# A hybrid encoder step on one core: the forget gate's running sums issued beside the first gate projection's blocks, and dense turns at 0.941 a step

## The chip, the cores and the metric

The kernel runs on one core of a Trainium2 chip. The metric is the device time of one execution in microseconds (us), lower is better. Before the change three runs took 1885.36, 1890.35 and 1894.71 us; the median is 1890.35 us.

The engines of the core appear under the names that the profile gives them: PE (matrix multiply, with PEld for its weight loads), DVE (vector), ACT (activation), POOL (the fourth compute engine) and SP, which here only starts DMAs. Each engine works off its own list of instructions in order; what one needs from another it waits for.

## The reference, cut to what matters

One layer of an encoder over 1024 prompt rows and 8 x 16 rows of running streams with 1024 cached rows each. All heads read one normalised input `u` through one combined projection:

```python
proj = jnp.einsum('bnd,de->bne', u, p['w_in'])
sq, sk, sv, fq, fk, fv, fg, z, xbc, dt = split_last(proj, IN_SIZES)
logf = jax.nn.log_sigmoid((fg + p['fox_b_f']).astype(jnp.float32))
# stick-breaking attention on sq, sk, sv
# forgetting attention ("FoX") on fq, fk, fv:
fcum = jnp.cumsum(logf, axis=1)                                     # prompt
fcum = jnp.cumsum(jnp.concatenate([past['fox_logf'], logf], axis=1), axis=1)   # streams
s = s + (fq_cum[..., :, None] - fk_cum[..., None, :])               # added to the scores before the softmax
# state-space mixer ("SSD") on z, xbc, dt; its output is gated:
ssd_o = rmsnorm(y * jax.nn.silu(z), p['ssd_norm_g'])
mix = jnp.concatenate([sb_o, fox_o, ssd_o], axis=-1)
out = jnp.einsum('bne,ed->bnd', mix, p['w_out'])
```

A cross-attention into 256 memory rows, a SwiGLU feed-forward and a last norm follow. The new keys, values, log gates and states are returned too. What the change touches is the running sum `fcum` of the log forget gates, and the time at which it is computed beside the projection of `z`.

## The kernel before, in words

A projection in this kernel is made of fp32 numbers split in a high and a low part; one product is three matmuls (`mm3`, L328, L329, L330). A block of weights is loaded by SP (L317) into a ring of four buffers `wr`, cast to its high part `wh` by ACT (L292), and its low part `wl` is subtracted by POOL in pieces of 256 columns (`pool_tt`, L132). L329 is the matmul of the three that reads `wl` in the projections whose weights are the moving operand.

Up to about 95 us of the span the kernel projects the memory rows and normalises the input; the first projections follow. From about 125 us to about 700 us runs the mixed stage, in which this change lies. It is written as generators that yield after a piece of work, a *turn*:

- `pipeline` (L629, called at L1297) makes one *step* for each unit of attention, 112 steps in all: 56 of stick-breaking attention, then 56 of FoX attention. A prompt unit of stick-breaking makes scores in pieces of up to 512 columns (PE L560, L561, and L563 for the mask), two sigmoids of each (ACT L519, L520), a running product over the whole row (DVE scan L522) and a product of the two (POOL L132, pieces of 256 columns, named `ws<-ws`). One step later the row is transposed (PE L578) and multiplied with the values (L593). A decode unit, for the running streams, loads cached keys (SP L882, into the same ring `wr`), transposes them (L888), multiplies (L873, L901, L902), and later transposes its weights (L924) and multiplies with the cached values (L933, L956).
- `fill_s` makes the *dense* turns: projections of FoX's queries and keys (12 turns; their matmuls have 384 columns), of its values and the forget gate (FV, 9 turns, 260 columns), the running sums (`fox_sums`, 4 turns), then what the list `ORD` names: `z0`, the first half of the gate z with dt (9 turns, 264 columns), `dt` (1), the xbc projection (24), and `z1` (9). That is 68 turns.
- At every step, `RATE[0]` is added to a counter and one dense turn is issued for each whole number in it (1.0 before). When the dense turns are used up, the SSD mixer's turns follow at `RATE[1]` = 1.1 a step.

The order in which the code issues instructions isn't yet the order on the engines: a scheduler sorts them for each engine by priority and by a model of when they could start. A step that is issued elsewhere can so move its instructions on all five engines.

`fox_sums` starts when FV has written the log gates' inputs `lf`. DVE and ACT compute the log of the gate (L400 to L413, L658), SP stores it (L660, L661) and loads the cached gates (L665), POOL makes three masks of ones and zeros in a buffer `sg` (L667 to L674), PE sums along the rows with them (L682, L683), transposes the sums (L690), sums over the chunks of the cache (L705 to L707) and spreads the result (L725). The sums go to memory (L692, L716, L718) and are read by the first FoX head and by the `z1` entry of `fill_s`, much later. PE's results lie in `psd`, a pool of two buffers, which FV's, z0's and xbc's blocks use too. `pad_cols` loads and transposes three old rows of the convolution's input (L782, L785); the first xbc turn reads them.

## Time and profile before

| | before |
|---|---|
| median of three runs | 1890.35 us |
| the profiled execution | 1894.55 us |
| its span | 1892.8 us |
| mean granted PE clock | 0.988 |
| PE busy | 97% of the span |
| DVE, ACT, POOL busy | 47%, 42%, 33% |
| DMA queues' share of 16 engines | 49.6% |

The profile is of one execution. Times in the timeline are counted from the span's start. A timeline row gives the start, the duration, the engine, the line, the operation with its tiles (out<-in), its shape and a count of equal instructions run together; in brackets stand the idle time ahead of it and what ended it. A table by windows gives for each stretch its width, the busy time and count of instructions of PE, PEld, DVE, ACT and POOL, then the granted PE clock (1.00 is full), the busy share of the DMA engines and GB/s. A fp32 matmul that isn't of the split kind is counted twice by the profile and once in the lists of the order below.

### The profile page before, as it was taken

The page shows a single profiled execution, that of the slowest core. Times are in us where ns is not written, and L with a number is a line of the kernel's source. Part 1 is how long each engine was busy: PE and PEld are TensorE (multiplying, and loading weights), DVE is VectorE, ACT ScalarE, POOL GpSimd, SP SyncE. Part 2 cuts the span into 40 slices and gives each one's busy share as a digit, 9 for nine tenths or more (in the row PEclk, how much of TensorE's full clock was granted, in tenths as well). Part 3 has the DMA queues.
Part 4 walks back from the last instruction along what each step waited for, and adds up shares of the span by engine and source line. Part 5 has one row for each costly group of instructions (what it writes and reads, how often), then busy time and mean ns, then how long its engine had stood idle before and what let it go on. Part 6 is the DMA issues. An engine that isn't in the chain of part 4 may idle for free.

```text
span 1892.8 us, 32368 instructions
## 1 busy us (share of the span) xinstructions
PE 1837.7 (97%) x12136; PEld 1638.6 (87%) x12136; DVE 886.4 (47%) x1798; ACT 802.1 (42%) x1719; POOL 617.9 (33%) x921
## 2 busy tenths in 40 slices
PE   7999999999999989999999989999999999999998
PEld 5899778888967767899988889999999999888886
DVE  3412323475656863444444586333333333455554
ACT  6522544545455862344332374333333333344443
POOL 7622425445115673111112107444444542000000
PEclk9999999999989999999999999999999999999999
DMA  9465654437587883245576124233322223657572
GB/s 338 145 189 149 206 142 133 147 109 207 179 249 228 282 290 102 108 134 173 173 271 219 56 81 112 75 87 79 76 71 70 70 70 105 207 187 243 174 243 89
DMA packets 291068, 296.64 MB, mean 157 GB/s; under 512 B 80092, under 2 KB 242884, under 8 KB 290912
## 3 DMA queue, kind: packets, MB, share of 16 engines
q1 hardware_dynamic: 290912, 294.57, 49.6%
q8 instruction: 96, 1.57, 0.3%
q14 instruction: 60, 0.49, 0.1%
HBM read 225.12 MB, written 69.91 MB: 156 GB/s over the span
## 4 chain that ended last, share of the span: by engine, by line
PE 83%; DMA 5%; DVE 4%; POOL 3%; ACT 3%; issue 2%; SPq 0%; DVEq 0%; POOLq 0%; ACTq 0%
PE psd L1868 11%; PE psd L328 10%; PE psd L329 10%; PE psd L330 10%; PE pst L1868 8%; PE pss L1868 4%; PE pss L328 3%; PE pss L330 3%; PE pss L329 3%; PE pso L1868 2%; POOL wl L132 2%; PE pst L328 1%; PE pst L329 1%; PE pst L330 1%; PE pso L593 1%
## 5 line engine op out<-in xcount | busy, mean ns | idle before, releaser
L132 POOL TENSOR_TENSOR wl<-wr,wh 128x256 fp32r<-128x256 f32 (+2 forms) x184 | 142.1, 805 | 233.0 <-ACT wh L292 232.8
L328 PE MATMUL psd<-act,wh 128*128 128x384 f32 x528 | 182.3, 345 | 0.0
L330 PE MATMUL psd<-act,wl 128*128 128x384 f32 x528 | 181.1, 343 | 0.6 <-POOL wl L132 0.6
L329 PE MATMUL psd<-act,wh 128*128 128x384 f32 x528 | 181.7, 344 | 0.0
L1868 PE MATMUL pst<-bT,tr 128*128 128x256 f32 (+1 forms) x1068 | 155.0, 293 | 0.0
L1868 PEld LDWEIGHTS pst<-bT,tr 128*128 128x128 f32 x1068 | 144.9, 188 | 0.1
L330 PE MATMUL psd<-wh,act 128*128 128x512 f32 (+3 forms) x424 | 136.9, 324 | 0.0
L329 PE MATMUL psd<-wl,act 128*128 128x256 f32 (+3 forms) x414 | 134.2, 325 | 2.7 <-POOL wl L132 2.7
L328 PE MATMUL psd<-wh,act 128*128 128x256 f32 (+3 forms) x414 | 133.3, 326 | 1.4 <-DMA act<-osc 1.0
L1868 PE MATMUL psd<-bT,tr 128*128 128x320 f32 (+1 forms) x912 | 132.8, 295 | 0.7 <-POOL tr L132 0.7
L1868 PEld LDWEIGHTS psd<-bT,tr 128*128 128x128 f32 x912 | 124.7, 188 | 1.0 <-POOL tr L132 0.9
L132 POOL TENSOR_TENSOR tr<-u,tr 128x256 fp32r<-128x256 f32 x110 | 82.6, 779 | 101.7 <-ACT tr L1704 83.8
L253 POOL TENSOR_SCALAR sm<-sm 128x1 f32<-128x1 f32 (+2 forms) x27 | 9.1, 338 | 297.3 <-ACT y L1970 207.8
L1843 DVE TENSOR_TENSOR tr<-tr,pst 128x256 f32<-128x256 f32 (+1 forms) x86 | 38.6, 449 | 139.9 <-ACT tr L1840 106.6
L330 PEld LDWEIGHTS psd<-act,wl 128*128 128x128 f32 x528 | 99.2, 188 | 3.2 <-issue 1.9
L132 POOL TENSOR_TENSOR ws<-ws 128x256 f32<-128x256 f32 (+2 forms) x100 | 69.3, 721 | 98.1 <-DVE ws L522 83.9
L328 PEld LDWEIGHTS psd<-act,wh 128*128 128x128 f32 x528 | 99.4, 188 | 2.2 <-issue 1.8
L329 PEld LDWEIGHTS psd<-act,wh 128*128 128x128 f32 x528 | 99.3, 188 | 1.9 <-issue 1.5
L132 POOL TENSOR_TENSOR tr<-raw,tr 128x256 fp32r<-128x256 f32 x94 | 69.2, 765 | 83.9 <-ACT tr L1704 75.7
L1704 ACT CAST tr<-tr 128x384 fp32r<-128x384 f32 (+1 forms) x70 | 37.6, 538 | 123.0 <-DMA tr<-hidsc 117.3
L329 PEld LDWEIGHTS psd<-wl,act 128*128 128x128 f32 x414 | 79.2, 191 | 10.9 <-POOL wl L132 4.0
L292 ACT CAST wh<-wr 128x512 fp32r<-128x512 f32 (+2 forms) x90 | 52.5, 622 | 81.7 <-PE psd L330 32.0
(643 smaller groups left out, 4730.5 us busy)
## 6 DMA issues: line engine op xcount, KB each, us to landing
u<-w_down SPq DMA_DIRECT2D x40, 512.0 KB
raw<-w_down SPq DMA_DIRECT2D x26, 512.0 KB
st<-qksc SPq DMA_DIRECT2D x48, 256.0 KB
wr<-w_in SPq DMA_DIRECT2D x44, 256.0 KB
tr<-hidsc SPq DMA_DIRECT2D x57, 192.0 KB
hidsc<-tr SPq DMA_DIRECT2D x34, 288.0 KB
qksc<-sg SPq DMA_DIRECT2D x48, 192.0 KB
wr<-cache_sb_k SPq DMA_DIRECT2D x32, 256.0 KB
```

Of the source, the lines that this page charges most:

```text
L132: POOL.tensor_tensor(out=out[:, a0:a1], in0=in0[:, a0:a1], in1=in1[:, a0:a1], op=op)
L253: POOL.tensor_scalar(v, ss, inv, EPS, ALU.mult, ALU.add)
L292: ACT.copy(hi, raw)
L328: PE.matmul(out, ah, bh, start=start, stop=False)
L329: PE.matmul(out, ah, bl, start=False, stop=False)
L330: PE.matmul(out, al, bh, start=False, stop=stop)
L593: return PE.matmul(po[r:r + 64, q_], vt[:, 2 * (k0 + i) + j, :], pfs[i][:, sl], start=start and k0 == 0 and (j == 0 or qp > 0), stop=k0 + ...
L1704: ACT.copy(hi, src)
L1843: DVE.tensor_tensor(out=at(out, g), in0=at(x, g), in1=ps[g][:, :GW[g]], op=op)
L1868: PE.matmul(dst[g][:, :GW[g]], x[:, ka], y[:, k, :], start=start and k == 0 and m == 0, stop=stop and k == 3 and m == 2, skip_group_check= ...
```

## The change

The dense rate goes from 1.0 to 0.941 turns a step. The running sums are no longer four turns of their own between FV and z0. They become a generator `sums`, and `beside` issues one of its turns behind each of the first four turns of z0. What is left of it (nothing, since z0 has nine turns) and `pad_cols` are issued ahead of the first xbc turn. There are now 64 dense turns, 4 fewer, and 64/68 = 0.941, so that the last of them falls on about the step it fell on before.

```diff
-RATE = (1.0, 1.1, 60)
+RATE = (0.941, 1.1, 60)
...
         yield from proj_v(1, C_FV, p_v[1], s_v[1], extra=4)
-        yield from fox_sums()
-        pad_cols()
+        sums = fox_sums()
+
+        def beside(gen):
+            for _ in gen:
+                next(sums, None)
+                yield
         for o in ORD:
...
             if o[0] == "z":
-                yield from z_proj(int(o[1]))
+                yield from beside(z_proj(int(o[1])))
             elif o == "dt":
                 dt_softplus()
                 yield
             else:
+                drain(sums)
+                pad_cols()
                 yield from xbc_proj(*o)
```

No instruction is added or taken away. The lists of the engines differ between about 150 us and 450 us of the span of before, a little between about 577 us and 705 us, and hardly anywhere else.

The first place is PE's list where FV begins. Rows read: line, operation, tiles out<-in, shape, and a count. `psd<-act,..` of 384 columns are the last turns of the projections ahead of FV, `psd<-wh,act` and `psd<-wl,act` of 260 columns are FV; `pst<-ident,ws` and `pso<-` belong to a decode unit, `pss<-` are scores. Before:

```order
L471 MATMUL pst<-ident,pt 128x128
L924 MATMUL pst<-ident,ws 128x128 x8
L471 MATMUL pst<-ident,pt 128x128 x2
L560 MATMUL pss<-st 128x128
L561 MATMUL pss<-st 128x128
L563 MATMUL pss<-mask_sb,identr 128x128
L560 MATMUL pss<-st 128x256
L561 MATMUL pss<-st 128x256
L563 MATMUL pss<-mask_sb,identr 128x128
L328 MATMUL psd<-wh,act 128x260
L924 MATMUL pst<-ident,ws 128x128
```

And with the change, from the last 384-column matmul on (the eight L924 stand 28 rows further up, and 24 matmuls of 384 columns and the ninth L924 between):

```order
L330 MATMUL psd<-act,wl 128x384
L560 MATMUL pss<-st 128x128
L561 MATMUL pss<-st 128x128
L563 MATMUL pss<-mask_sb,identr 128x128
L560 MATMUL pss<-st 128x256
L561 MATMUL pss<-st 128x256
L563 MATMUL pss<-mask_sb,identr 128x128
L933 MATMUL pso<-pt,so 32x128 x4
L933 MATMUL pso<-vr,st 32x128 x32
L328 MATMUL psd<-wh,act 128x260
L329 MATMUL psd<-wl,act 128x260
```

FV's first matmul now stands behind the last dense turn of the keys and behind a decode unit's product with the cached values (L933), which stood behind it.

The second place is PE's list between FV's end and the second block of z0 (264 columns). Before, the sums of the gates come first:

```order
L902 MATMUL pss<-st 32x128 x4
L690 MATMUL psd<-ident,fqc 4x128 x8
L593 MATMUL pso<-pt,st 64x256 x4
L560 MATMUL pss<-st 128x512
L561 MATMUL pss<-st 128x512
L560 MATMUL pss<-st 128x384
L561 MATMUL pss<-st 128x384
L563 MATMUL pss<-mask_sb,identr 128x128
L705 MATMUL psd<-so,sg 128x4
L706 MATMUL psd<-fold,so 32x16
L707 MATMUL psd<-sg,so 32x16
L593 MATMUL pso<-pt,st 64x256
```

L682 and L683 stand a few rows ahead of L902 there, L725 and L785 some rows behind, then the first block of z0. With the change, the first block of z0 starts right behind L902, with scores and L593 between its matmuls, and this stands between the first block's end and the second block:

```order
L924 MATMUL pst<-ident,ws 128x128 x5
L560 MATMUL pss<-st 128x384
L561 MATMUL pss<-st 128x384
L563 MATMUL pss<-mask_sb,identr 128x128
L560 MATMUL pss<-st 128x512
L561 MATMUL pss<-st 128x512
L563 MATMUL pss<-mask_sb,identr 128x128
L560 MATMUL pss<-st 128x512
L561 MATMUL pss<-st 128x512
L682 MATMUL psd<-lf,sg 128x32
L683 MATMUL psd<-so,sg 128x28
L328 MATMUL psd<-wh,act 128x264
```

Ahead of the first row shown stand two more pieces of scores, of 128 and 256 columns, and four L924. The first turn of the sums, L682 and L683, now stands ahead of z0's second block; L690, L705 to L707 and L725 stand ahead of its third, fourth and fifth block.

The third place is POOL's list, from the masks of the sums to the products of the scores. Before, the masks (`sg`) come ahead of z0's weights (`wl`, four times a row of 256 x2 and one of 16):

```order
L132 TENSOR_TENSOR ws<-ws 128x255
L667 MEMSET sg 128x384
L668 AFFINE_SELECT sg<-sg 128x128
L672 AFFINE_SELECT sg<-sg 128x128
L674 AFFINE_SELECT sg<-sg 128x128
L132 TENSOR_TENSOR wl<-wr,wh 128x256 x2
```

With the change they come behind them, and behind products of scores too; these rows follow on the last of z0's `wl`:

```order
L132 TENSOR_TENSOR ws<-ws 128x256 x4
L132 TENSOR_TENSOR ws<-ws 128x127
L132 TENSOR_TENSOR ws<-ws 128x256 x3
L132 TENSOR_TENSOR ws<-ws 128x127
L863 MEMSET st 128x128
L132 TENSOR_TENSOR ws<-ws 128x256 x3
L132 TENSOR_TENSOR ws<-ws 128x255
L132 TENSOR_TENSOR ws<-ws 128x127
L667 MEMSET sg 128x384
L869 COPY st<-st 64x2x16 x4
L132 TENSOR_TENSOR ws<-ws 128x255
L668 AFFINE_SELECT sg<-sg 128x128
```

The mask that L682 reads (L668) thus moved from ahead of z0's weights to behind them and 15 products of scores. On SP the load of the cached gates and the two stores of the log gate, which stood ahead of and among z0's weight loads, moved behind them, and the cached keys of a decode unit (L882) moved from behind three stores to ahead of them.

## The prediction

> **What bounds the kernel now.** I read the page's busy shares first, then a table by windows around the places where the change moves work, then PE's waits in those windows, then the timeline at each wait.

> ```profile
> PE 1837.7 (97%) x12136; PEld 1638.6 (87%) x12136; DVE 886.4 (47%) x1798; ACT 802.1 (42%) x1719; POOL 617.9 (33%) x921
> ...
> 150.00:222.00 72.00, 71.61 (x446) 65.25 (x446) 21.44 (x25) 30.42 (x68) 21.31 (x37) 1.00 0.68 200
> 222.00:232.00 10.00, 7.35 (x71) 6.15 (x73) 4.45 (x7) 4.54 (x13) 9.42 (x19) 0.83 0.38 112
> 232.00:267.00 35.00, 35.00 (x317) 32.15 (x306) 6.37 (x14) 12.21 (x29) 9.07 (x18) 1.00 0.39 119
> 267.00:292.00 25.00, 19.42 (x122) 13.30 (x121) 14.01 (x43) 16.64 (x36) 13.52 (x17) 0.82 0.84 216
> 292.00:316.00 24.00, 22.14 (x223) 20.07 (x222) 7.81 (x15) 9.54 (x24) 15.72 (x28) 0.97 0.38 113
> ...
> 577.00:712.00 135.00, 124.51 (x1053) 95.80 (x1052) 97.80 (x260) 91.45 (x201) 87.51 (x139) 1.00 0.81 273
> ```

> PE is the bound. The change adds and removes no instruction, so all that it can win or lose is time in which PE idles or runs at a lower clock. The first number after the comma in a window is PE's busy time, and the width less that is its idle time: 0.39 us in 150 to 222, 2.65 at FV's start (222 to 232), 0 in 232 to 267, 5.58 in the stretch of the running sums (267 to 292) and 1.86 at z0's first blocks. From 455 to 577 the order on PE is the same in both, and behind 712 too. So some 8 us of idle time in two stretches are in play, and beside them the clock, 0.83 and 0.82 there.

> ```profile
> 269.00:272.90 3.90, 1.46 (x12) 0.43 (x11) 2.94 (x17) 2.24 (x6) 0.00 (x0) 0.98 0.75 231
> 272.90:276.20 3.30, 3.04 (x15) 2.64 (x14) 2.01 (x13) 1.26 (x3) 0.00 (x0) 0.50 0.75 211
> 286.30:293.10 6.80, 6.52 (x28) 5.16 (x28) 5.70 (x7) 3.54 (x8) 6.80 (x7) 0.51 1.04 287
> ```

> In the stretch of the sums PE ran at half clock twice, for 3.3 us and 6.8 us. The matmuls there would have taken half as long at full clock: (3.04 + 6.52)/2 = 4.8 us is the most that the clock cost. The stretch ahead of the first, 3.9 us with 1.46 busy, shows what came before it.

> [...]

> **The change part by part.**

> *FV's start.* What PE waits for there:

> ```profile
> PE psd L329 <- POOL wl L132: 2.2, 2, 2.0
> ...
> 217.09 0.34 PE L330 MATMUL psd<-act,wl 128*128 128x384 f32 x1
> ...
> 220.77 0.34 PE L330 MATMUL psd<-act,wl 128*128 128x384 f32 x1
> ...
> 221.06 1.13 PE L924 MATMUL pst<-ident,ws 128*128 128x128 f32 x8
> ...
> 222.17 0.31 PE L560 MATMUL pss<-st 128*128 128x128 f32 x1
> ...
> 222.88 0.33 PE L328 MATMUL psd<-wh,act 128*128 128x260 f32 x1
> ...
> 226.62 0.39 PE L329 MATMUL psd<-wl,act 128*128 128x260 f32 x1 [2.02 <-POOL wl L132]
> ...
> 230.21 0.65 PE L933 MATMUL pso<-pt,so 128*32 128x128 f32 x8
> 230.64 2.49 PE L933 MATMUL pso<-vr,st 128*32 128x128 f32 x64
> 233.06 0.39 PE L329 MATMUL psd<-wl,act 128*128 128x260 f32 x1
> ...
> 222.28 2.55 POOL L132 TENSOR_TENSOR ws<-ws 128x256 f32<-128x256 f32 x4 [5.95 <-PE pst L924]
> 224.78 2.60 POOL L132 TENSOR_TENSOR wl<-wr,wh 128x256 fp32r<-128x256 f32 x3
> 227.33 0.20 POOL L863 MEMSET st<- 128x128 f32 x1
> 227.49 1.58 POOL L132 TENSOR_TENSOR wl<-wr,wh 128x256 fp32r<-128x256 f32 x3
> ...
> 229.39 0.75 POOL L869 COPY st<-st 64x32 f32<-64x32 f32 x4
> ```

> PE transposes a decode unit's weights (L924), which lets POOL go on: four products (2.55), then FV's low parts (2.60), and L329 waits 2.02 us for the first. In the changed order FV's first L328 no longer stands 1.8 us behind the start of L924. Between them lie 24 matmuls of 384 columns, 0.175 each (217.09 to 220.77 holds 21 of them), so 4.2 us; the two short score pieces, 0.7 (222.17 to 222.88); and the decode unit's product, 2.85 (230.21 to 233.06): 7.8 us. POOL needs at most 2.55 + 2.60 for products and low parts, and 0.95 for a memset and copies that may slip ahead (0.20 and 0.75, L863 and L869): 6.1 us. Both waits of L329 go, 2.2 us; the clock that fell with it comes back, 10 x (1 - 0.83) = 1.7 at most, of which I take 1.3 because not all of that window was busy. Sum **-3.5 us**; bounds 0 (something else is late, the cast for instance) and -4.35 (all idle and all clock).

> *From FV's end to z0's second block.* FV ends at F = 267.0 (ACT reads its last block at 267.07). Two of PE's waits in 267 to 292, the largest and that of the sums, and the timeline:

> ```profile
> PE pst L888 <- DMA wr<-cache_sb_k: 2.1, 2, 1.9
> ...
> PE psd L705 <- ACT xc L691: 0.6, 1, 0.6
> ```

> ```profile
> 267.07 0.37 ACT L488 COPY so<-psd 128x256 f32<-128x256 f32 x1 [2.50 <-PE psd L330]
> ...
> 268.88 0.58 SPq L665 DMA_DIRECT2D sg<-cache_fox_logf  x1
> 269.56 1.34 SPq L882 DMA_DIRECT2D wr<-cache_sb_k  x3
> ...
> 275.14 0.46 SPq L660 DMA_DIRECT2D p_fox_logf<-lf  x1
> 275.65 0.75 SPq L661 DMA_DIRECT2D s_fox_logf<-lf  x1
> ...
> 277.31 3.14 POOL L132 TENSOR_TENSOR wl<-wr,wh 128x256 fp32r<-128x256 f32 x6 [28.66 <-ACT wh L292]
> 281.63 7.31 POOL L132 TENSOR_TENSOR wl<-wr,wh 128x256 fp32r<-128x256 f32 x6 [1.17 <-ACT wh L292]
> 288.94 6.93 POOL L132 TENSOR_TENSOR ws<-ws 128x256 f32<-128x256 f32 x9
> 295.98 2.43 POOL L132 TENSOR_TENSOR ws<-ws 128x256 f32<-128x256 f32 x4
> ...
> 279.38 1.03 PE L690 MATMUL psd<-ident,fqc 128*4 128x128 f32 x8
> ...
> 282.73 2.72 DVE L522 TENSOR_TENSOR_SCAN ws<-ws 128x1152 f32<-128x1152 f32 x1 [4.91 <-ACT ws L519]
> ...
> 289.25 1.02 PE L785 MATMUL psd<-ident,xc 24*128 24x24 f32 x8
> ...
> 295.65 0.37 PE L329 MATMUL psd<-wl,act 128*128 128x264 f32 x1
> ```

> The sums' own waits are short (0.6 for L705); the stretch is a lean one because z0's weights arrive late: POOL stood still for 28.66 us until the first came, and had the last low part at 281.63 + 7.31 = 288.94, F + 21.9. z0's second block began at 295.65, **F + 28.65**. The sums filled that gap. In the changed order PE starts z0's first block instead and takes its low parts as they come, with scores between. SP no longer has L660, L661 and L665 ahead of and among the weight loads (0.46 + 0.75 + 0.58), and the load of cached keys (1.34) is moved ahead of stores, so the loads can come up to 3.1 us earlier. The first low part then starts at F + 7.2 instead of F + 10.3. I put the last one between F + 13.5 (twelve pieces at the 0.52 us of the first group, 3.14/6) and F + 18.8 (everything as slow as before, 3.1 earlier): F + 16.5, a little nearer the second, because DVE's scans run beside it as before.

> What is late next is the masks. L682 now stands ahead of the second block, and needs L668, behind 15 products of scores that follow the last low part on POOL. A product costs 0.61 (2.43/4) to 1.22 (a piece of the 281.63 row, 7.31/6), and 0.77 (6.93/9) in the longest group of products. The 15 with the memsets, copies and L668 itself (about 1.3) make 10.5 us at 0.61, 12.9 at 0.77 and 19.6 at 1.22; I take 11.8, between the two measured on products. With 0.5 for L682 and L683 the second block then begins at 16.5 + 11.8 + 0.5 = **F + 28.8**. Queued behind L682 on PE is all of z0 but its first block, and behind that the xbc projection. By then PE has done five more score pieces than before at that point, 1792 columns, at the 0.7 us for 384 of the two short ones some 3 us; and it has not yet done the rest of the sums and L785 (1.03 for L690, 1.02 for L785, about as much again at L690's price for the smaller ones between: 3 us). These cancel. So the region comes out at **0**: the stall is moved, not removed. Its bounds: -9 us, when all 5.6 us of idle and some 3.5 of the clock go because the masks come in time; and +8, when the products take 1.22 each (19.6 us for all).

> *Later sums.* L690, L705 to L707 and L725 share the two `psd` buffers with z0's blocks, so each waits until a block has been read, and z0's next block waits until DVE or ACT has read the sums' tile. A scan on DVE can stand ahead of that (2.72 at 282.73). Three such tiles could cost 0 to 8 us; score work at hand covers most, I take 0.5 us inside the zero above.

> *Rationing.* Up to FV, 21 turns at 0.941 come up to one step later. In 150 to 222 PE is busy 71.61 of 72.00 us with the same work in another order: **0**. If that cover goes, a missing turn leaves a hole of 24 x 0.175 = 4.2 us. `pad_cols` and its load move ahead of xbc, some 40 us later; its eight transposes (about 1 us) and its DMA lie beside z0's work and are due only there. The SSD turns start about a quarter of a turn later; 577 to 712 has 10.49 us idle, which such shifts move by up to 4 us either way, and I take 0.

> **Sum**: -3.5 + 0 + 0 = -3.5 us against the profiled execution of 1894.55 (span 1892.8). The median of the runs shown is 1890.35, 4.2 below it; on that the forecast is **1887 us**. A measurement of this kernel tells about 0.5%, 9.45 us, from no change.

> **The rivals.**

> *Both stalls go.* If z0's low parts are there at F + 13.5 and POOL's pieces run at the undisturbed 0.52, L668 is done at 13.5 + 7.8 + 1.3 = F + 22.6, and scores and z0's first block keep PE at work for most of that time: the 5.6 us of idle and 3.5 of the clock go, -3.5 - 9 = -12.5, **1878**. For it: the gap is filled with z0's own matmuls and PE is the bound. Against it: the 15 products ahead of L668 and only about 3 us of scores ahead of L682. Chance 0.20.

> [...] Chance 0.08. [...]

> *Slower: the masks hold z0.* L682 waits on POOL while z0's weights lie ready. At 1.22 us a product, as in the row at 281.63, the second block begins at 16.5 + 19.6 + 0.5 = F + 36.6, and a half clock behind the gap adds 1.5 (as at 272.90, half of 3.04): 9.5 us later than before. With POOL and DVE that far behind, the later sums' tiles wait too, half of the 8 us above: -3.5 + 9.5 + 4 = +10, **1900**. It outweighs FV's gain once a product takes about 1 us on average, and shows in a measurement at 1.2. For it: DVE scans and POOL products share this stretch, as they did at 281.63. Against it: the groups at 288.94 and 295.98 ran at 0.61 to 0.77. Chance 0.15.

> *The change does little of what it says.* The scheduler could have sorted the sums back ahead of z0; the order shows that it hasn't on PE, so this holds no chance of its own.

> **How the numbers follow.** Forecast 0.57, clock rival 0.08 (also within 0.5%), both stalls gone 0.20, masks hold z0 0.15. Faster by over 0.5% 0.20, within 0.5% 0.65, slower by over 0.5% 0.15. The range reaches down past the 1878 of the faster case, by 2 us for a 577-to-712 window that comes out better, and up to the +8 of the region on the forecast, 1895, with 3 us for that window: 1876 to 1898; only the slower rival's 0.15 lies outside.

> **What would show it.** In the profile of the changed kernel: L329's wait for POOL `wl` at FV's start is gone (right) or still near 2 us (wrong). PE idles between z0's first and second block, with L682 waiting for POOL `sg` L668, and the second block begins about 28.8 us behind FV's end; if it begins at 18 to 20, the first rival holds, at 38, the slower one. [...] The window of the pipeline's end (577 to 712 before) keeps about 10.5 us of idle. The prediction is wrong if a stage behind 712 us differs by more than 1 us, or if `psd` buffers make z0's blocks wait more than 3 us in all.

## The result and the profile after

| | before | with the change |
|---|---|---|
| median | 1887.86 us (6 runs, 1881.97 to 1894.71) | 1905.13 us (6 runs, 1899.74 to 1906.31) |
| ratio | | 1.0091, 95% interval 1.0071 to 1.0112 |
| the profiled execution | 1894.55 us | 1906.31 us |
| its span and mean PE clock | 1892.8 us, 0.988 | 1904.6 us, 0.985 |

The change makes the kernel slower by 17 us; 1887 was forecast, from 1876 to 1898. PE's busy time hardly changed, so the loss is idle time and clock, as the prediction held, but at other places than it held. This is the page's row of busy times after, and then the table by windows, cut at the same events in both kernels: from 95 us to FV's first L330 (the third matmul of its first product), the rest of FV, FV's end to z0's end, the xbc projection, and from there to the SSD turns' end. First before, then after (width, then busy time and count of PE, PEld, DVE, ACT, POOL, the granted PE clock, DMA share, GB/s).

```profile
PE 1839.1 (97%) x12136; PEld 1642.2 (86%) x12136; DVE 891.7 (47%) x1798; ACT 803.8 (42%) x1719; POOL 621.5 (33%) x921
```

```profile
95.00:226.80 131.80, 128.95 (x849) 121.96 (x849) 31.98 (x43) 49.68 (x111) 38.51 (x62) 1.00 0.63 188
226.80:267.00 40.20, 40.01 (x361) 36.50 (x362) 7.44 (x15) 13.30 (x31) 13.97 (x31) 0.96 0.39 117
267.00:334.40 67.40, 59.96 (x485) 49.90 (x484) 24.43 (x67) 29.78 (x69) 29.60 (x45) 0.92 0.51 140
334.40:488.60 154.20, 151.41 (x1063) 135.70 (x1063) 95.30 (x147) 76.29 (x175) 71.33 (x96) 1.00 0.52 152
488.60:728.90 240.30, 227.55 (x1757) 176.35 (x1756) 155.00 (x435) 139.06 (x308) 104.17 (x175) 0.96 0.74 241
```

```profile
95.00:224.80 129.80, 129.80 (x917) 123.29 (x917) 31.26 (x43) 50.35 (x111) 43.21 (x68) 1.00 0.62 188
224.80:262.90 38.10, 38.05 (x306) 35.02 (x304) 8.96 (x17) 15.33 (x36) 12.59 (x21) 1.00 0.46 140
262.90:337.60 74.70, 60.71 (x452) 50.53 (x453) 25.55 (x65) 28.31 (x65) 30.68 (x48) 0.84 0.43 121
337.60:504.70 167.10, 158.77 (x1085) 141.59 (x1084) 95.53 (x148) 76.85 (x176) 69.91 (x97) 0.97 0.49 141
504.70:741.90 237.20, 221.66 (x1757) 173.82 (x1756) 158.09 (x435) 138.58 (x308) 106.11 (x175) 0.99 0.76 244
```

Idle time is width less PE's busy time. What the clock cost is put at half of PE's busy time in the stretches granted at 0.50. That is an estimate, a little high: eight matmuls of L1132 (256 columns) took 1.06 us at full clock (before, at 543.05) and 1.92 at half (562.48), so 45% of the 1.92 was lost. Here are two of these stretches of the kernel before, ahead of FV's end and in the SSD stretch (the two in z0's stretch, which cost 4.9 us by the exact cuts, stand in the prediction with 4.8), and then those of the changed kernel:

```profile
228.40:231.80 3.40, 3.40 (x41) 3.03 (x43) 0.28 (x1) 1.09 (x2) 3.28 (x10) 0.50 0.56 152
556.10:576.60 20.50, 20.50 (x77) 12.67 (x75) 10.38 (x35) 10.45 (x21) 3.35 (x6) 0.50 0.70 203
...
276.60:283.40 6.80, 5.82 (x24) 5.43 (x24) 1.64 (x2) 3.06 (x8) 6.80 (x12) 0.50 0.57 149
286.90:297.10 10.20, 6.12 (x21) 4.80 (x22) 8.64 (x28) 1.92 (x4) 7.05 (x16) 0.50 0.10 11
310.80:317.60 6.80, 4.96 (x46) 4.23 (x46) 1.11 (x5) 2.59 (x5) 2.72 (x4) 0.50 0.34 84
362.00:365.40 3.40, 3.40 (x14) 3.17 (x12) 1.78 (x2) 1.84 (x3) 2.37 (x2) 0.50 0.85 273
396.10:402.90 6.80, 5.58 (x21) 5.59 (x22) 4.27 (x7) 3.50 (x8) 6.80 (x9) 0.50 0.53 159
...
682.80:686.20 3.40, 3.35 (x13) 3.11 (x14) 2.75 (x9) 3.40 (x8) 1.88 (x4) 0.50 1.05 363
```

In the changed kernel the first three cost (5.82 + 6.12 + 4.96)/2 = 8.5 us of z0's stretch and the next two 4.5 us of the xbc stretch; the last and one more like it, at 566.8, cost 3.4 us of the SSD stretch. Idle time and clock together make this account, in us (differences and sums are taken before rounding):

| stretch | before | after | difference |
|---|---|---|---|
| 95 us to FV's end | 4.7 | 0.0 | -4.7 |
| FV's end to z0's end | 7.4 + 4.9 = 12.3 | 14.0 + 8.5 = 22.5 | +10.2 |
| xbc | 2.8 | 8.3 + 4.5 = 12.9 | +10.1 |
| to the SSD turns' end | 12.8 + 10.2 = 23.0 | 15.5 + 3.4 = 18.9 | -4.1 |

The four differences add up to 11.5 us; the profiled spans differ by 11.8. So FV's gain came, and twice 10 us were lost behind it, half of them in a stretch that the prediction didn't price at all. Most of the -4.1 comes from a stretch of half clock from 556 to 576 us in the profile of before, which cost 10.2 us; all the half clock of the profile after in this stage cost 3.4. Both profiles taken of before have it (e8) and were 1894.55 and 1895.37 us, while the median is 1887.86. This fits the two profiled executions differing by 12 us only and the medians by 17; what the clock did in the runs without a profile is known as a mean alone.

Where z0's stretch loses, in the timeline after (SP, POOL, DVE, then PE):

```profile
260.27 2.21 SPq L882 DMA_DIRECT2D wr<-cache_sb_k  x4
...
264.25 4.03 SPq L317 DMA_DIRECT2D wr<-w_in  x8
...
306.01 2.01 SPq L942 DMA_DIRECT2D vr<-cache_sb_v  x2
...
269.01 10.26 POOL L132 TENSOR_TENSOR wl<-wr,wh 128x256 fp32r<-128x256 f32 x12 [12.33 <-ACT wh L292]
...
291.42 0.29 POOL L668 TENSOR_SCALAR_AFFINE_SELECT sg<-sg 128x128 f32<-128x128 f32 x1
...
292.28 0.20 DVE L658 SCALAR_TENSOR_TENSOR lf<-lf,sg 128x36 f32<-128x36 f32 x1
...
274.49 0.39 PE L329 MATMUL psd<-wl,act 128*128 128x264 f32 x1 [1.36 <-POOL wl L132]
...
277.58 0.59 PE L329 MATMUL psd<-wl,act 128*128 128x264 f32 x1 [1.89 <-POOL wl L132]
...
290.21 0.79 PE L560 MATMUL pss<-st 128*128 128x512 f32 x1 [2.21 <-ACT ws L520]
...
292.62 0.61 PE L682 MATMUL psd<-lf,sg 128*128 128x32 f32 x2 [1.19 <-DVE lf L658]
...
294.36 0.57 PE L328 MATMUL psd<-wh,act 128*128 128x264 f32 x1
...
312.19 1.72 PE L933 MATMUL pso<-vr,st 128*32 128x128 f32 x28 [3.46 <-DMA vr<-cache_sb_v]
```

The reader is to see a chain. Four blocks of cached keys go into the ring `wr` first and z0's weights behind them, at 264.25. POOL's low parts follow at 269.01 to 279.27, and z0's first block waits for them (1.36, 1.89). Two of these twelve pieces took 2.49 and 2.46 us, the others 0.2 to 0.75; while those two ran, DVE worked off two scans (L522, 271.67 to 276.33). PE goes on to the scores that stand behind that block and waits for them too (2.21); L682 waits for the log of the gate on DVE, done at 292.48, not for the mask, done at 291.71. z0's second block begins at 294.36. Ahead of z0's fourth block and behind it stand the two halves of a decode unit's product with the cached values. The second half waits 3.46 us for its values: their load starts at 306.01, when the first half has been done, and now only the 24 matmuls of that block stand between the halves. Before, nine matmuls of scores stood there as well, from 303.16 on, and no wait showed:

```profile
300.24 0.81 SPq L942 DMA_DIRECT2D vr<-cache_sb_v  x2
...
303.16 0.28 PE L560 MATMUL pss<-st 128*128 128x256 f32 x1
...
305.29 1.08 PE L933 MATMUL pso<-vr,st 128*32 128x128 f32 x32
```

Those nine filled 2.1 us. Most of the rest of the 3.46 lies in the load: before, the second half ran 5.0 us after the load's start without a wait, after 6.2 us with one.

### The profile page after: what moved, and what is told of

Read it like the earlier page. It is cut to its first block, busy times and chain, and to the rows that moved or that the text cites. A ratio compares the mean times of both kernels' runs of the same rounds, so it can differ in the third digit from the quotient of the medians.

```text
span 1904.6 us, 32357 instructions
## 1 busy us (share of the span) xinstructions
PE 1839.1 (97%) x12136; PEld 1642.2 (86%) x12136; DVE 891.7 (47%) x1798; ACT 803.8 (42%) x1719; POOL 621.5 (33%) x921
## 4 chain that ended last, share of the span: by engine, by line
PE 67%; DMA 4%; DVE 4%; issue 2%; POOL 1%; ACT 1%; SPq 0%; DVEq 0%; POOLq 0%; ACTq 0%
PE psd L1874 11%; PE pst L1874 9%; PE psd L328 6%; PE psd L329 6%; PE psd L330 6%; PE pss L1874 4%; PE pss L328 3%; PE pss L330 3%; PE pss L329 3%; PE pso L1874 2%; PE pst L328 1%; PE pst L329 1%; PE pst L330 1%; DMA act<-acsc 1%; DMA wr<-cache_fox_k 1%
## 5 line engine op out<-in xcount | busy, mean ns | idle before, releaser
L132 POOL TENSOR_TENSOR wl<-wr,wh 128x256 fp32r<-128x256 f32 (+2 forms) x184 | 140.6, 797 | 242.6 <-ACT wh L292 242.6
L328 PE MATMUL psd<-act,wh 128*128 128x384 f32 x528 | 183.6, 348 | 0.8 <-ACT wh L292 0.8
L330 PE MATMUL psd<-act,wl 128*128 128x384 f32 x528 | 182.2, 345 | 1.1 <-POOL wl L132 1.1
L329 PE MATMUL psd<-act,wh 128*128 128x384 f32 x528 | 183.0, 347 | 0.0
L329 PE MATMUL psd<-wl,act 128*128 128x256 f32 (+3 forms) x414 | 134.9, 327 | 3.8 <-POOL wl L132 3.8
L330 PE MATMUL psd<-wh,act 128*128 128x512 f32 (+3 forms) x424 | 137.1, 324 | 0.0
L328 PE MATMUL psd<-wh,act 128*128 128x256 f32 (+3 forms) x414 | 133.6, 326 | 0.8 <-DMA act<-osc 0.7
L132 POOL TENSOR_TENSOR tr<-u,tr 128x256 fp32r<-128x256 f32 x110 | 82.4, 778 | 101.9 <-ACT tr L1710 88.0
L132 POOL TENSOR_TENSOR ws<-ws 128x256 f32<-128x256 f32 (+2 forms) x100 | 73.2, 760 | 103.9 <-DVE ws L522 90.2
L330 PEld LDWEIGHTS psd<-act,wl 128*128 128x128 f32 x528 | 100.0, 189 | 3.8 <-issue 1.9
L328 PEld LDWEIGHTS psd<-act,wh 128*128 128x128 f32 x528 | 100.3, 190 | 2.9 <-issue 1.2
L329 PEld LDWEIGHTS psd<-act,wh 128*128 128x128 f32 x528 | 100.3, 190 | 1.4 <-issue 0.9
L132 POOL TENSOR_TENSOR tr<-raw,tr 128x256 fp32r<-128x256 f32 x94 | 69.2, 765 | 84.5 <-ACT tr L1710 76.3
L329 PEld LDWEIGHTS psd<-wl,act 128*128 128x128 f32 x414 | 79.6, 192 | 13.5 <-POOL wl L132 6.5
L292 ACT CAST wh<-wr 128x512 fp32r<-128x512 f32 (+2 forms) x90 | 52.3, 621 | 90.4 <-PE psd L330 32.7
```

Of the source, the lines that this page charges most:

```text
L132: POOL.tensor_tensor(out=out[:, a0:a1], in0=in0[:, a0:a1], in1=in1[:, a0:a1], op=op)
L292: ACT.copy(hi, raw)
L328: PE.matmul(out, ah, bh, start=start, stop=False)
L329: PE.matmul(out, ah, bl, start=False, stop=False)
L330: PE.matmul(out, al, bh, start=False, stop=stop)
```

## The experiments

All ratios below are to runs of the kernel before taken beside each experiment on the same chip (medians 1887.0 to 1890.1 us). The four numbers of idle time and clock are those of the account: to FV's end, z0, xbc, and to the SSD turns' end; before has 4.7, 12.3, 2.8, 23.0, the change 0.0, 22.5, 12.9, 18.9. Each comes from one profile; the second profile of before (e8) has 4.0, 13.0, 2.6, 24.2, so differences of about 1 us mean nothing.

**e1, the sums beside z0 without rationing.**

```diff
-RATE = (0.941, 1.1, 60)
+RATE = (1.0, 1.1, 60)
```

> The sums beside z0 as in the change, but the dense rate stays at 1.0, so FV and z0 start at the steps of before. Theory A (the loss is the place of the sums: their first turn stands between z0's first two blocks in PE's list and waits there for DVE's log chain and POOL's masks, and their stores hold up a decode unit's load of cached values on SP): FV's gain is missing too, so about 10 to 20 us slower than before; PE waits for the sums' inputs inside z0. Theory B (the loss is the rationing: at 0.941 the attention units run ahead of the dense turns, so that a decode unit's keys, its products on POOL and z0's and xbc's weights meet): same as before or up to 10 us faster, FV's wait of 2 us still there, z0 without a wait over 2 us.

Measured: 1896.7 us, ratio 1.0053 (1.0033 to 1.0073). Stretches 3.9, 6.4, 5.6, 31.8. Neither theory: z0's stretch is 6 us better than before, so the place beside z0 is not a loss in itself; the time goes in the SSD stretch, which starts four turns early here.

**e2, rationing without the sums beside z0** (before, with `RATE = (0.941, 1.1, 60)`).

> The dense rate of 0.941 with the sums in turns of their own as before; the 68 dense turns end about four steps later than before and the SSD turns lose about four steps. Theory A: the gain at FV's start stays (4 to 5 us), no wait of z0's second block on the sums, so 5 us faster than before, less what the later SSD turns cost: within 5 us of before either way. Theory B: 10 to 17 us slower, with the loss between 290 and 410 us of the span as in the changed kernel.

Measured: 1911.3 us, ratio 1.0121 (1.0097 to 1.0146). Stretches 0.2, 7.1, 11.4, 38.9. The gain to FV's end came here too, so the rationing gives it without the sums beside z0. The time is longer than either theory had it: the 68 turns end four steps late, and the end of the stage pays.

**e3, the first turn of the sums alone, ahead of z0.**

```diff
-RATE = (0.941, 1.1, 60)
+RATE = (0.956, 1.1, 60)
...
         sums = fox_sums()
+        next(sums)
+        yield
```

> As the change, but the first turn of the sums (log chain, masks, the first two matmuls) is a turn of its own ahead of z0, and the rate is 65/68 = 0.956; only the three later turns stand beside z0's blocks. In POOL's list the masks are back ahead of z0's low parts. Theory A with the first turn as the cause: the wait of 1 to 2 us at L682 and the stretch of half clock around it go, 8 us or more of the 17 come back: at most 9 us slower than before. Theory A with the later turns (stores ahead of the load of cached values on SP) as the cause: the wait of PE for the cached values of about 3.5 us stays, 10 to 15 us slower. Theory B: 15 us slower as in the change.

Measured: 1894.1 us, ratio 1.0041 (1.0027 to 1.0054). Stretches 0.0, 13.8, 7.2, 19.2. Ten of the 17 us come back, but the run changes the steps at which all later turns fall as well.

**e4, rationing until FV's end, then 1.029** (sums in turns of their own).

```diff
-RATE = (1.0, 1.1, 60)
+RATE = (0.941, 1.1, 1.029)
...
         yield from proj_v(1, C_FV, p_v[1], s_v[1], extra=4)
+        fv[0] = True
...
-        acc += RATE[1] if done[0] else RATE[0]
+        acc += RATE[1] if done[0] else RATE[2] if fv[0] else RATE[0]
```

> The sums in turns of their own as before; the dense rate is 0.941 until FV's last turn and 1.029 from then on, so that the dense turns end at the step of before. Theory A: the gain at FV's start without a loss: 4 to 6 us faster than before. Theory B: the attention units are as far ahead of z0 at its start as with 0.941 throughout, so about 5 to 10 us slower than before, with the loss at z0 and the first xbc turns.

Measured: 1898.7 us, ratio 1.0059 (1.0040 to 1.0078). Stretches 0.0, 9.6, 7.7, 33.4. FV's gain is there, and is more than lost later, most of it in the SSD stretch, where neither theory had put it.

**e5, the sums' part ahead of z0's block in each shared turn** (`beside` calls `next(sums, None)` first, then advances `gen`).

> The change with one thing turned round: in each shared turn the sums' part is issued ahead of z0's block, not behind it; rates as in the change. L682 then stands ahead of z0's first block on PE, and the masks ahead of z0's low parts on POOL. Theory A (the place of the first part behind z0's first block, where five pieces of scores are used up while PE waits, and nothing is left to cover the load of cached values): idle and half clock from FV's end to z0's end fall from 22 us to about 13, in all 6 to 9 us slower than before. Theory B (rationing alone): 15 us slower or more, as the change.

Measured: 1902.8 us, ratio 1.0114 (1.0079 to 1.0150). Stretches 0.0, 17.8, 12.7, 18.2. z0's stretch gained 4.7 us, less than theory A wanted, and the time 2 us. So the place of the first part is at most a part of the cause. PE now waits longer for the cached values than in the change:

```profile
PE pso L933 <- DMA vr<-cache_sb_v: 5.4, 1, 5.4
```

**e6, the masks built ahead of z0** (the memset and the three selects issued behind FV's last turn).

> The change, with the three masks of the sums built on POOL ahead of z0 (as soon as FV's turns are issued); the order of PE stays, but for L682 a few rows earlier. If POOL's masks held L682 up: the wait of PE between z0's first two blocks goes and 5 us or more of the 17 come back. If PE's order is the cause and the masks were ready at about the time that PE came: the same as the change within 3 us, with L682 waiting for DVE or for nothing.

Measured: 1904.8 us, ratio 1.0107 (1.0087 to 1.0126). Stretches 0.0, 21.6, 12.4, 15.5. The same as the change: the masks, on which the prediction let the stall hang, don't hold it up. L682 (line 687 in this kernel) now waits 4.58 us for DVE:

```profile
292.65 0.64 PE L687 MATMUL psd<-lf,sg 128*128 128x32 f32 x2 [4.58 <-DVE lf L672]
```

These six and the trace of e7 led to a third theory, C. At a rate of 1.0 with the sums beside z0 (e1, e7), SP issues z0's weight loads ahead of a decode unit's keys (all eight of them by the timelines, not half); at 0.941 z0's first turn comes a step later and its weights stand behind the keys. The next runs turn that order round. They don't turn it round alone: with it, z0's turns move by a step against the attention units.

**e7, rationing only behind z0.**

```diff
-RATE = (0.941, 1.1, 60)
+RATE = (1.0, 1.1, 0.895)
...
                 yield from beside(z_proj(int(o[1])))
+                z0[0] = True
...
-        acc += RATE[1] if done[0] else RATE[0]
+        acc += RATE[1] if done[0] else RATE[2] if z0[0] else RATE[0]
```

> The sums beside z0 as in the change, dense rate 1.0 until z0's last turn and 0.895 from then on, so that the dense turns end at the step of before. Theory A': sums beside z0 are a gain where z0 starts at the step of before (idle and half clock to z0's end 6 us as with the rate of 1.0 throughout, against 12 before), and what made that kernel slow was the dense turns' earlier end: then 0 to 6 us faster than before. Theory B (any rationing of dense turns costs in the xbc stretch, where decode units and weights meet): 5 to 10 us slower than before, with over 7 us of idle and half clock in the xbc stretch.

Measured: 1892.4 us, ratio 1.0029 (1.0011 to 1.0047). Stretches 1.1, 4.8, 4.9, 26.5. Both theories missed the time: z0's stretch is as good as theory A' had it, but the run is some 5 us slower than before. SP in this kernel issues z0's eight loads from 226.06 on, 38 us earlier than in the change; then follows the table by windows of z0's and the xbc stretch:

```profile
226.06 3.23 SPq L317 DMA_DIRECT2D wr<-w_in  x4
...
233.62 0.89 SPq L317 DMA_DIRECT2D wr<-w_in  x2
235.18 0.88 SPq L317 DMA_DIRECT2D wr<-w_in  x2
...
266.41 1.98 SPq L882 DMA_DIRECT2D wr<-cache_sb_k  x4
```

```profile
264.50:321.00 56.50, 51.74 (x457) 43.47 (x456) 24.06 (x66) 28.27 (x65) 26.61 (x45) 1.00 0.50 146
321.00:481.20 160.20, 155.33 (x1091) 138.97 (x1092) 96.19 (x154) 76.94 (x178) 71.96 (x95) 1.00 0.53 150
```

**e8, the kernel before once more**, for its profile.

> The kernel before, unchanged, for a second profile: if the half clock of 20 us at 556 us of the span in its first profile is an accident of that execution, it is shorter here and the span some 5 to 7 us less; if it belongs to the kernel, it is there again.

Measured: 1895.37 us, clock 0.988. The half clock is there again, 17 us of it:

```profile
561.00:578.00 17.00, 17.00 (x64) 10.24 (x64) 6.93 (x22) 7.76 (x15) 4.36 (x8) 0.50 0.71 212
```

So it is no accident of one profile. But the 72 runs of before taken beside the experiments have a median clock of 0.991 and a median of 1887.7 us, and the ten at 0.988 or below took 1889.8 to 1899.1 us. Most of them thus had less half clock than the two profiles, though their records don't say where.

**e9, e7 with one empty turn ahead of z0.**

```diff
-RATE = (1.0, 1.1, 0.895)
+RATE = (1.0, 1.1, 0.919)
...
         sums = fox_sums()
+        yield
```

> As the run that rations only after z0 (the best so far of those with the sums beside z0), with one empty turn ahead of z0 and 0.919 afterwards, so that the dense turns end at the same step. In the order the only thing that this turns round at z0's start is which comes first into the shared buffers wr: SP loads five blocks of a decode unit's cached keys ahead of z0's weights, as in the change, where it loaded half of z0's weights ahead of them. Theory C (that order is what the rationing turned round, and it makes the loss at z0): idle and half clock from FV's end to z0's end rise from 5 us to 15 to 22 us, and the time to 1900 us or more. Rationing by itself (theory B): no rationing ahead of z0 here, so 5 to 9 us there and 1892 us, as without the empty turn.

Measured: 1910.3 us, ratio 1.0128 (1.0113 to 1.0143). Stretches 2.6, 20.7, 4.0, 29.7, as theory C has it. One step, and z0's stretch loses 16 us more than in e7, without any rationing ahead of it. SP's rows show the keys first again, and the table 17.1 us in one piece at half clock:

```profile
268.70 1.50 SPq L882 DMA_DIRECT2D wr<-cache_sb_k  x3
270.29 0.90 SPq L317 DMA_DIRECT2D wr<-w_in  x2
...
266.80:340.70 73.90, 58.21 (x458) 47.66 (x457) 27.98 (x66) 28.88 (x67) 31.02 (x48) 0.88 0.45 124
...
291.60:308.70 17.10, 9.94 (x39) 8.05 (x38) 11.40 (x33) 4.00 (x9) 10.75 (x23) 0.50 0.11 12
```

**e10, FV late and z0's weights early.**

```diff
-RATE = (0.941, 1.1, 60)
+RATE = (0.941, 1.1, 1.15, 0.905)
...
+        part[0] = 1
         yield from proj_v(1, C_FV, p_v[1], s_v[1], extra=4)
+        part[0] = 2
...
-        acc += RATE[1] if done[0] else RATE[0]
+        acc += RATE[1] if done[0] else RATE[(0, 2, 3)[part[0]]]
```

> The sums beside z0 as in the change; the dense rate is 0.941 until FV begins, 1.15 until FV's last turn and 0.905 from then on. FV then begins late, as in the change, and z0's first weights are loaded ahead of the decode unit's keys. Theory C: FV's 4 to 5 us and z0's 7 us are both gained; 3 to 9 us less in the xbc and SSD stretches; 1880 to 1888 us, 0 to 7 us faster than before. Theory B: as slow as the change within 5 us.

Measured: 1888.0 us, ratio 1.0001 (0.9988 to 1.0013). Stretches 1.5, 4.6, 8.8, 24.7. All 17 us come back, at the slow end of what theory C had, and without a gain over before:

```profile
263.20:320.70 57.50, 52.91 (x463) 44.46 (x462) 23.44 (x66) 28.21 (x65) 26.00 (x47) 1.00 0.56 154
320.70:483.40 162.70, 157.32 (x1085) 139.90 (x1083) 94.40 (x146) 75.63 (x175) 67.94 (x97) 0.98 0.51 146
```

**e11, the sums as four turns of their own behind z0** (rate 1.0, 68 turns).

> Before, with the four turns of the sums and the convolution's rows moved behind z0 as turns of their own; rate 1.0, 68 turns. z0's weights are again ahead of the keys. Theory C: idle and half clock from FV's end to z0's end about 5 us in place of 12, and the sums' four turns, now behind z0 where scores and xbc's weights lie, cost less than the 7 us gained: 2 to 7 us faster than before. If the sums have to stand beside z0's blocks for the gain: same as before or slower, since the four lean turns only move.

Measured: 1902.8 us, ratio 1.0082 (1.0065 to 1.0099). Stretches 4.3, 9.0, 16.2, 22.6. z0's stretch gained some, the xbc stretch lost 13 us: the lean turns only moved.

**e12, the change with one empty turn ahead of dt and xbc** (0.97 from z0's end on).

> The change up to z0's end, then one empty turn ahead of the dt and xbc turns, and 0.97 instead of 0.941 from there, so that the dense turns end at the same step. The stretch from FV's end to z0's end has to lose 20 to 23 us to idle and half clock, as in the change. The xbc stretch lost 12.9 us in the change and 2.8 before. If that hangs on which xbc turn falls beside which decode unit (theory P), one step's shift brings it down to 3 to 8 us and the time to 1896 to 1901 us. If it hangs on the thinner dense work of a step or is what z0's delay leaves behind (theory R), it stays at 11 to 14 us and the time within 3 us of the change's 1905.

Measured: 1903.6 us, 1900.1 to 1908.4, ratio 1.0074 (1.0050 to 1.0098). Stretches 0.0, 23.0, 8.4, 18.1. The stretch moved in the profile as theory P has it, though 8.4 is just outside its 3 to 8; the time moved by less than its spread and fits theory R: inconclusive.

**e13 and e14, e10 with one and two empty turns ahead of dt and xbc** (0.927 and 0.948 from FV's end on).

> The kernel with FV late and z0's weights early, with one empty turn ahead of dt and xbc and 0.927 from z0 on, so that the dense turns end at the same step. Nothing changes up to z0's end (6 us or less of idle and half clock there). Theory P (the xbc stretch's loss hangs on which xbc turn falls beside which decode unit): its 8.7 us move by 3 us or more, and the time with them, to 1882 to 1886 us if it falls as it did in the change. Theory R (the loss is what a delay at z0 or a thinner step leaves): it stays within 2 us, and the time at 1886 to 1890 us.

> As the run with one empty turn ahead of dt and xbc, with two and 0.948. Theory P: again another loss in the xbc stretch, by 2 us or more, in either direction. Theory R: within 2 us of 8.7, and the time at 1886 to 1890 us.

Measured: e13 1887.0 us, ratio 0.9990 (0.9969 to 1.0011), stretches 1.3, 6.0, 2.9, 24.4; e14 1894.9 us, ratio 1.0038 (1.0021 to 1.0056), stretches 3.6, 7.4, 10.6, 24.9. The xbc stretch of both, e13 first:

```profile
322.80:480.30 157.50, 154.61 (x1086) 137.54 (x1085) 93.38 (x149) 77.04 (x181) 69.47 (x97) 1.00 0.54 154
```

```profile
326.10:492.30 166.20, 159.75 (x1092) 142.19 (x1091) 96.36 (x149) 77.84 (x180) 69.86 (x97) 0.97 0.50 145
```

The stretch loses 8.8, 2.9, 10.6 us with no, one and two empty turns. In e13 it moves as theory P has it, but the time is in theory R's range; in e14 the move is 1.9 us, just within theory R's 2, but the time is not. So the stretch, one profile each, speaks for which xbc turn falls beside which decode unit and not for thinner steps; the times don't settle it. No version tried beats the kernel before beyond its measurement.

## Why the prediction was wrong, step by step

*FV's start, -3.5.* Right, with its mechanism: 4.7 us to FV's end became 0.0, and e2 and e4 show that the rationing does it without the sums beside z0. The wait of L329 is gone. It isn't the only way there: e7, without rationing ahead of FV, lost only 1.1 us, and e14, with it, 3.6.

*Rationing up to FV, 0.* Right: PE is busy all 129.80 of 129.80 us.

*z0's low parts at F + 16.5, its second block at F + 28.8.* F is 262.9 now. The last low part came at 279.27, F + 16.4. The block began at 294.36, F + 31.5; the late one was the log of the gate on DVE, 0.8 us later than the mask that was named. e6 shows that the mask's place costs nothing. That the forecast F + 28.8 came so near was luck.

*"These cancel. So the region comes out at 0."* **This step failed.** It stopped at the second block's start and took a piece of scores done early to be worth as much as one done later. It is not: PE used up five pieces ahead of L682, and nine matmuls of scores were missing where the load of cached values then stood bare (3.46 us). The clock behind the gaps was half for 23.8 us of this stretch, at a cost of 8.5, where the prediction had put in the 4.8 that it had read before and no more. The stretch lost 22.5 us and not 12.3. That the five pieces would have covered the load is read from the trace and not shown: e5, which takes the sums' first part ahead, waited 5.4 us there. What goes with the loss in the runs is an order that the prediction had read and priced as a small gain: cached keys ahead of z0's weights in the shared ring. This is what the runs show of it, idle time and clock in z0's stretch, by the order on SP:

| | z0's weights first | a decode unit's keys first |
|---|---|---|
| sums beside z0 | e1 6.4, e7 4.8, e10 4.6, e13 6.0, e14 7.4 | change 22.5, e3 13.8, e5 17.8, e6 21.6, e9 20.7, e12 23.0 |
| sums in turns of their own | e11 9.0 | before 12.3, e4 9.6, e2 7.1 |

Before has the keys first too. With the keys first, the sums' four turns are worth having as turns: attention goes on while z0's weights travel. With the weights first they aren't needed. The rationing turned the order round by one step (e7 against e9), and so the two halves of the change, each with something to give, spoil each other. That z0 must not come that step later, with the sums beside it, is shown by e9 and e10; that the order of the loads is the reason, and not the attention unit beside which z0's turns then fall, was not tried by itself.

*xbc: `pad_cols` hidden, no other term.* **The second step that failed**, by leaving a stretch out: it lost 10 us more than before. At its worst place DVE works off a turn's convolution (L771, L772) and scans ahead of the decode unit's L952, and PE waits for that; DVE's rows, then PE's:

```profile
394.64 1.68 DVE L771 SCALAR_TENSOR_TENSOR xc<-xc,cols 128x1024 f32<-128x1024 f32 x1
396.25 0.81 DVE L772 SCALAR_TENSOR_TENSOR sg<-sg,cols 128x128 f32<-128x128 f32 x1
396.98 0.28 DVE L952 SCALAR_TENSOR_TENSOR so<-pso,maskh 128x128 f32<-128x128 f32 x1
...
397.32 0.69 PE L956 MATMUL pst<-fold,so 128*128 128x64 f32 x2 [2.45 <-DVE so L952]
```

e12, e13 and e14 suggest that the stretch hangs on the step at which the turns fall. That this queue on DVE is the way was read from the trace and not tried by itself, so the cause of these 10 us stays open.

*The end of the stage, 0 within 4.* Its idle time rose by 2.8 us; its clock can't be compared, for the reason given with e8. Why it loses 15 to 39 us in the runs stays open; in e1 and e2 the dense turns end at another step. From the SSD turns' end to the end of the span the time is 1163.9 us before and 1162.7 after, a little over the 1 us that the prediction allowed; no run gives a reason.

*The rivals.* The slower one had the right sign and the wrong mechanism: nine products on POOL took 7.06 us, or 0.78 each, and the masks were not late. That its 9.5 us for z0 is near the measured 10.2 is luck. Its price of 1.22 is no product's: in the row at 281.63 four pieces of 256 columns took 0.72 or 0.73 each, and two of 16 columns took 2.47 and 2.15. No run shows the condition on which the clock rival (0.08) had the changed stretch keep its clock: half clock cost 8.5 us in z0's stretch and 4.5 in the xbc stretch, and ahead of three of the drops PE was busy for a quarter to two fifths of the time:

```profile
273.20:276.60 3.40, 1.21 (x7) 0.62 (x7) 3.40 (x3) 1.62 (x5) 3.40 (x2) 1.00 1.05 279
...
392.70:396.10 3.40, 0.79 (x5) 0.41 (x3) 3.40 (x4) 1.62 (x3) 3.40 (x4) 1.00 0.03 7
307.40:310.80 3.40, 1.33 (x12) 1.12 (x10) 0.00 (x0) 0.00 (x0) 0.00 (x0) 1.00 0.86 280
```

## What to carry to other kernels

When work is moved so that it fills one gap, ask what it covered where it stood, and follow the stretch to the next point where both orders have done the same, not to the first gap's end. Where two streams load through one ring of buffers, look at which is issued first: one empty turn ahead of z0, which turned that order round and moved z0 by a step, was worth 18 us here (e7, e9). An account of idle time and lost clock by stage, cut at the same events in both kernels, finds the places; the causes need runs of their own.

## What the runs showed of the hardware

A piece of work on POOL took far longer beside a long scan on DVE. A subtraction of 16 columns took 0.22 us by itself (before, at 278.69); beside scans of 2.72 and 2.00 us (before, from 282.73 and 286.91) two took 2.47 and 2.15 us and ended with the scan, and in the changed kernel one took 2.49, beside a scan of 2.75 us from 271.67.
